# Seven-product steps in 68 of the 264 block steps of two FFN products

## The chip, the cores and the metric

The kernel runs on one core of one Trainium2 chip. The metric is the device time of one execution in microseconds. In the views of the profile PE is TensorE (matrix products), PEld its loading of the stationary operand, DVE VectorE, ACT ScalarE, POOL GpSimd, and SP the queue from which transfers are issued. PSUM is the memory in which TensorE accumulates: eight banks of 128 partitions by 512 float32.

## The reference, cut to what matters

One decoder layer on 256 tokens of 2048 features, all in float32: a feed-forward part (FFN), a token mixer, a second FFN, and a last normalization.

```python
def swiglu(h, w_in, w_out):
    gu = h @ w_in                                   # 2048 -> 2 * 5632
    gate, up = gu[..., :D_FF], gu[..., D_FF:]
    return (jax.nn.silu(gate) * up) @ w_out         # 5632 -> 2048
...
    h = h + 0.5 * swiglu(rmsnorm(h, ffn1_norm[l]), ffn1_w_in[l], ffn1_w_out[l])
    u = rmsnorm(h, mix_norm[l]) @ w_in_mix[l]
    ...                                             # pooling and gated linear attention
    h = h + jnp.concatenate([y_pool, y_gla], axis=-1) @ w_out_mix[l]
    h = h + 0.5 * swiglu(rmsnorm(h, ffn2_norm[l]), ffn2_w_in[l], ffn2_w_out[l])
return rmsnorm(h, final_norm)
```

The weights are 334 MB read once, and nearly all of the arithmetic is in the FFNs' products.

## The kernel before, in words

**A product in three matmuls.** A float32 operand is written as hi + lo, two values of a reduced float32 type (fp32r in the profile), and a product of two blocks is hi·hi + hi·lo + lo·hi, three matmuls that add up in PSUM. The activations are stationary (128 features by 128 tokens), the weights stream past them 512 columns at a time. So each pair of a 128-row tile of weights and a tile of 128 tokens costs three matmuls per 512 columns. There are two token tiles (t = 0, 1).

**Weights.** `weights` (L69) loads two row tiles (K tiles) by 512 columns, 512 KB, on SP's queue (L73); ScalarE rounds them to hi (L86, the tile `wh_...`), VectorE subtracts for lo (L87, `wl_...`); raw, hi and lo have four buffers each. `project` (L98) runs over the eight such groups of a 2048-row product, and for each group does the first token tile's six matmuls and then the second's six (L110), into one PSUM bank per token tile (`ps_acc`, four banks, so two products alternate).

**FFN in.** `ffn_in` (L210) runs over 11 chunks of 512 hidden columns: the gate product (names f1g, f2g), ScalarE's SiLU of it (L226), the up product (f1u, f2u), VectorE's gating (L234, tile `f1a`), eight TensorE transposes into the PSUM tile `f1tp` (L240, one of four banks of `ps_t`), and the split into hi (L242) and lo (L243). All 11 chunks' results are kept in SBUF.

**FFN out.** `residual` (L250) then runs, for each of four blocks of 512 output columns, over all 44 row tiles of w_out, adds half the result to the residual stream h (L262), and transposes h for the next stage; the tiles are called `wh_h`, `ps_h` here for the FFNs as for the mixer's output product. In the last block of the second FFN the last six groups are done for the first token tile first, and then for the second in halves of 256 columns, so that the final normalization of the first overlaps (`finish`, L588 to L632).

**The mixer** between the FFNs has products of the same kind (mgr, mk, mq, mv, mg, mp) with small matrix work between. It starts with the gate product mgr of 336 columns, whose result is needed for a chain of small steps before the key product mk ends.

**Order.** Each engine runs its instructions in a fixed order of its own and waits for semaphores. That order is set when the kernel is built, by a scheduler that simulates the engines' timeline and lets each engine take an instruction that is ready; the program's order is its guide. So the order in the code and the order on an engine can differ.

At the start, x comes transposed, row tile by row tile with the first weights.

## Time and profile before

| | |
|---|---|
| time, median of 3 runs | 1782.69 us (1782.53 to 1784.28) |
| profiled execution: first to last instruction (span) | 1780.9 us, 20687 instructions |
| the profiled execution's own time beside the median | its span is 1.8 us under the median |
| mean granted TensorE clock | 0.999 |
| TensorE busy | 1768.4 us, 99% |
| TensorE weight load | 1467.1 us, 82% |
| VectorE busy | 894.8 us, 50% |
| ScalarE busy | 791.2 us, 44% |
| GpSimd busy | 35.1 us, 2% |
| DMA | 338.01 MB, mean 190 GB/s; the main queue's packets took 59.5% of the engines' span |

By the chain of waits the stages are: first FFN in 4.8 to 502 us, out to 739.5; mixer to 1003.5, its output product to about 1048.6; second FFN in to 1537, out to 1772; the end to 1780.9.

A row of a group reads: source line, engine, operation, output <- inputs, partitions x elements, type, xcount | busy us, mean ns of one | idle us of the engine just before them, and what ended it. A row of the timeline or of the chain starts with the start and the length in us. Loading a weight overlaps the matmul before it, so TensorE's busy time is not the number of matmuls times the time of one alone.

### The profile page before, as it was taken

What the parts mean: (1) busy time and instruction counts of PE and PEld (TensorE: products, weight loads), DVE (VectorE), ACT (ScalarE), POOL (GpSimd) and SP (SyncE); (2) the same over time, 40 slices, a digit from 0 to 9 for tenths busy, and PEclk for the clock granted to TensorE, in tenths of its full rate; (3) what the DMA queues carried; (4) which work ended last, traced back from release to release, by engine and by line L of the source; (5) the groups of instructions that cost most, each with busy time, mean ns of one, the idle gap of its engine ahead of it and who ended that gap; (6) DMA issues with size and microseconds to landing.
All of it is one profiled execution on the core that took longest, in us unless ns stands there. A gap on an engine that the chain in (4) does not pass through costs nothing.

```text
span 1780.9 us, 20687 instructions
## 1 busy us (share of the span) xinstructions
PE 1768.4 (99%) x8086; PEld 1467.1 (82%) x8086; DVE 894.8 (50%) x902; ACT 791.2 (44%) x911; POOL 35.1 (2%) x40
## 2 busy tenths in 40 slices
PE   9999999999999999999999999999999999999998
PEld 6888888888888888878978888888888888888886
DVE  5544444444555445544455554444444555554454
ACT  6444444444444444454445544444444444443443
POOL 0000000000000000000010000000000000200000
PEclk9999999999999999999999999999999999999999
DMA  9666666666565655555554566666666666766653
GB/s 310 202 189 189 189 190 189 189 189 189 190 190 190 197 190 189 175 171 171 173 193 145 188 188 189 189 190 189 189 189 189 189 189 190 215 194 193 192 196 133
DMA packets 176449, 338.01 MB, mean 190 GB/s; under 512 B 10807, under 2 KB 19255, under 8 KB 176096
## 3 DMA queue, kind: packets, MB, share of 16 engines
q1 hardware_dynamic: 174976, 333.10, 59.5%
q0 software_dynamic: 944, 3.06, 0.6%
q8 instruction: 63, 1.03, 0.2%
q10 hardware_dynamic: 432, 0.55, 0.1%
q14 instruction: 34, 0.28, 0.0%
HBM read 334.56 MB, written 2.10 MB: 189 GB/s over the span
## 4 chain that ended last, share of the span: by engine, by line
PE 98%; issue 0%; DMA 0%; DVE 0%; ACT 0%; SPq 0%; POOLq 0%; POOL 0%; DVEq 0%
PE ps_h L110 31%; PE ps_f2g L110 13%; PE ps_f2u L110 13%; PE ps_f1u L110 13%; PE ps_f1g L110 13%; PE ps_mp L110 3%; PE ps_mv L110 2%; PE ps_mg L110 2%; PE ps_mk L110 1%; PE ps_mq L110 1%; PE ps_mgr L110 1%; PE f2tp L240 1%; PE f1tp L240 1%; PE tp_h L203 0%; DMA wr_f1g<-in_ffn_w_in 0%
## 5 line engine op out<-in xcount | busy, mean ns | idle before, releaser
L87 DVE TENSOR_TENSOR wl_h<-wr_h,wh_h 128x1024 fp32r<-128x1024 f32 x208 | 256.8, 1236 | 269.9 <-ACT wh_h L86 269.7
L86 ACT CAST wh_h<-wr_h 128x1024 fp32r<-128x1024 f32 x208 | 218.9, 1054 | 301.4 <-PE ps_h L110 274.5
L87 DVE TENSOR_TENSOR wl_f2u<-wr_f2u,wh_f2u 128x1024 fp32r<-128x1024 f32 x88 | 107.8, 1225 | 131.5 <-ACT wh_f2u L86 131.5
L87 DVE TENSOR_TENSOR wl_f1u<-wr_f1u,wh_f1u 128x1024 fp32r<-128x1024 f32 x88 | 107.8, 1225 | 129.2 <-ACT wh_f1u L86 129.1
L87 DVE TENSOR_TENSOR wl_f2g<-wr_f2g,wh_f2g 128x1024 fp32r<-128x1024 f32 x88 | 107.8, 1225 | 102.1 <-ACT wh_f2g L86 102.1
L87 DVE TENSOR_TENSOR wl_f1g<-wr_f1g,wh_f1g 128x1024 fp32r<-128x1024 f32 (+1 forms) x89 | 108.0, 1213 | 98.9 <-ACT wh_f1g L86 98.5
L86 ACT CAST wh_f2g<-wr_f2g 128x1024 fp32r<-128x1024 f32 x88 | 92.8, 1055 | 126.8 <-PE ps_f2u L110 66.6
L86 ACT CAST wh_f2u<-wr_f2u 128x1024 fp32r<-128x1024 f32 x88 | 92.7, 1053 | 122.6 <-PE ps_f2u L110 66.9
L86 ACT CAST wh_f1g<-wr_f1g 128x1024 fp32r<-128x1024 f32 (+1 forms) x89 | 93.0, 1045 | 119.1 <-PE ps_f1u L110 63.2
L86 ACT CAST wh_f1u<-wr_f1u 128x1024 fp32r<-128x1024 f32 x88 | 92.6, 1052 | 116.1 <-PE ps_f1u L110 61.9
L110 PE MATMUL ps_f1g<-wh_f1g,xT_hi 128*128 128x512 f32 x352 | 137.1, 394 | 2.5 <-ACT xT_hi L142 2.4
L110 PE MATMUL ps_h<-wh_h,f2hi 128*128 128x512 f32 (+1 forms) x364 | 139.2, 382 | 0.0
L110 PE MATMUL ps_h<-wh_h,f2lo 128*128 128x512 f32 (+1 forms) x364 | 139.1, 382 | 0.0
L110 PE MATMUL ps_h<-wl_h,f2hi 128*128 128x512 f32 (+1 forms) x364 | 139.1, 382 | 0.0
L110 PE MATMUL ps_f2g<-wh_f2g,h_hi 128*128 128x512 f32 x352 | 138.0, 392 | 0.0
L110 PE MATMUL ps_h<-wh_h,f1hi 128*128 128x512 f32 x352 | 137.3, 390 | 0.0
L110 PE MATMUL ps_h<-wl_h,f1hi 128*128 128x512 f32 x352 | 137.2, 390 | 0.0
L110 PE MATMUL ps_f2g<-wh_f2g,h_lo 128*128 128x512 f32 x352 | 137.1, 389 | 0.0
L110 PE MATMUL ps_f2g<-wl_f2g,h_hi 128*128 128x512 f32 x352 | 137.1, 389 | 0.0
L110 PE MATMUL ps_h<-wh_h,f1lo 128*128 128x512 f32 x352 | 137.0, 389 | 0.0
L110 PE MATMUL ps_f1u<-wl_f1u,xT_hi 128*128 128x512 f32 x352 | 136.9, 389 | 0.0
L110 PE MATMUL ps_f1u<-wh_f1u,xT_lo 128*128 128x512 f32 x352 | 136.9, 389 | 0.0
(225 smaller groups left out, 3323.8 us busy)
## 6 DMA issues: line engine op xcount, KB each, us to landing
wr_h<-in_ffn_w_out SPq DMA_DIRECT2D x176, 512.0 KB, 3.9
wr_f1u<-in_ffn_w_in SPq DMA_DIRECT2D x88, 512.0 KB, 3.5
wr_f2g<-in_ffn_w_in SPq DMA_DIRECT2D x88, 512.0 KB, 3.4
wr_f2u<-in_ffn_w_in SPq DMA_DIRECT2D x88, 512.0 KB, 3.4
wr_f1g<-in_ffn_w_in SPq DMA_DIRECT2D x87, 512.0 KB, 3.5
wr_h<-in_w_out_mix SPq DMA_DIRECT2D x32, 512.0 KB, 4.0
wr_mv<-in_w_in_mix SPq DMA_DIRECT2D x16, 512.0 KB, 3.6
wr_mp<-in_w_in_mix SPq DMA_DIRECT2D x16, 512.0 KB, 4.5
```

Source lines behind the costliest of these rows:

```text
L86: nc.scalar.copy(out=hi[:, :n, :cw], in_=raw[:, :n, :cw])
L87: nc.vector.tensor_tensor(out=lo[:, :n, :cw], in0=raw[:, :n, :cw], in1=hi[:, :n, :cw].bitcast(F32), op=ALU.subtract,)
L110: nc.tensor.matmul(ps[t][:, c], a[:, s], b[:, j, c], start=kt == first and i == 0, stop=kt == last and i == 2, skip_group_check=c.start > 0,)
L240: nc.tensor.transpose(tp[:, k, :], a[:, k * P : (k + 1) * P], ident)
```

## The change

**What a step is.** The FFN products are cut into steps of two token tiles (A's rows) by two K tiles by two column blocks of 512. In FFN-in the two column blocks are the gate's and the up's block of the same chunk; in FFN-out they are two neighbouring blocks of output columns. A has four blocks a(t, k), B four blocks B11, B12, B21, B22 (K tile, column block). The host lays the weights out by steps, each 1 MB in one piece, in the order B11, B12, B22, B21; `load` fetches one step, with three buffers for the raw data. Everything split out of it lies in one pool of 14 pair tiles (two blocks of 512, hi or lo).

**S and W.** An S step is the eight block products as before, 24 matmuls. A W step (the Strassen form with seven products, in Winograd's arrangement) makes sums of the blocks ahead: S1 = A21 + A22, S2 = S1 - A11, S3 = A21 - A11, S4 = A12 - S2; T1 = B12 - B11, T3 = B12 - B22, T2 = B22 - T1, T4 = B21 - T2. Its seven products, 21 matmuls, go to different places. A12·B21, S4·B22 and A22·T4 are added to the group's ordinary sums. A11·B11, S2·T2, S3·T3 and S1·T1 collect in four PSUM banks of their own over all W steps of a group; at the end of the W steps `combine` adds them up in SBUF (one ScalarE copy, four VectorE sums over 512).

The T blocks are made by VectorE in the raw tile itself, in three instructions, and all but one of the seven blocks of weights are split in pairs. The S blocks of x and of the mixer's result are made once per FFN (four K pairs); those of the hidden activations from the transposes in PSUM.

**Where.** Each FFN runs in three slabs of 4, 4 and 3 chunks: first the in-products of the slab's chunks, then the slab's part of the out-product, in two halves of 1024 columns that are added into h. In chunks 1, 3, 5, 7 and 9 the eight steps are S W S W S W W S; the out halves have 3 and 2, 3 and 2, 2 and 2 W. That makes 34 W per FFN, 68 of 264 steps.

**PSUM.** A group (one chunk's in-product, or one half of a slab's out-product) takes four banks for its sums and, if it has W, the other four for its partials; groups change sides. The transposes of a chunk go to the side of its own sums.

**The rest.** The mixer's weights come in pieces of four K tiles; mgr and mk are both done to their half first, then mgr ends, the small steps start, and mk ends. The transfers of pscale, gnorm, tri, walpha, band, w_pool and the final gains are issued on SP's queue instead of GpSimd's. In the last group of the second FFN the last two steps (four K tiles, twice as many columns) are done for one token tile first instead of the last six groups of two K tiles. At the start x comes in pairs of row tiles (256 KB) and the first step's weights in four pieces.

Names: f is the first FFN, z the second; i the in-product, o the out-product. `ps_fi3` holds the sums of chunk 3, `wr_fi3_4`, `wh_fi3_4_1`, `wl_fi3_4_1` are the raw, hi and lo data of K pair 4 (piece 1), `pw_` the partials, `add_` the combined ones. `ps_fo0_0` is the out group of the slab that starts with chunk 0, left half; `wh_fo0_2` its row pair 2. The lines below are those of the changed kernel.

```diff
+SLABS = ((0, 1, 2, 3), (4, 5, 6, 7), (8, 9, 10))
+W_PAIRS = (1, 3, 4, 6)
+PLAIN = "SSSSSSSS"
+MIXED = "SWSWSWWS"
+MIXED_CHUNKS = (1, 3, 5, 7, 9)
+OUT = {                                    # (chunk of the slab, K pair, kind), left and right half
+    4: (
+        ((0, 0, "S"), (0, 1, "S"), (1, 0, "W"), (2, 0, "S"), (1, 1, "W"), (3, 0, "S"), (2, 1, "W"), (3, 1, "S")),
+        ((0, 0, "S"), (0, 1, "S"), (2, 0, "S"), (1, 0, "W"), (3, 0, "S"), (1, 1, "W"), (2, 1, "S"), (3, 1, "S")),
+    ),
...
+}
+RAW_BUFS = 3
+UNIT_BUFS = 14
...
+    def split_to(hi, lo, src):
+        nc.scalar.copy(out=hi, in_=src)
+        nc.vector.tensor_tensor(out=lo, in0=src, in1=hi.bitcast(F32), op=ALU.subtract)
...
+    def w_step(src, name):
+        raw = load(src, name=name)
+        w = raw.rearrange("p (b c) -> p b c", c=CW)
...
+        split_to(h_hi, h_lo, w[:, 0, :])
+        b_hi, b_lo = split_pair(w[:, 2:4, :], f"{name}_1")
         nc.vector.tensor_tensor(
-            out=lo[:, :n, :cw],
-            in0=raw[:, :n, :cw],
-            in1=hi[:, :n, :cw].bitcast(F32),
+            out=w[:, 0:2, :], in0=w[:, 1:2, :].broadcast_to([P, 2, CW]), in1=w[:, 0:4:2, :],
             op=ALU.subtract,
         )
+        nc.vector.tensor_tensor(out=w[:, 2, :], in0=w[:, 2, :], in1=w[:, 0, :], op=ALU.subtract)
+        t_hi, t_lo = split_pair(w[:, 0:2, :], f"{name}_2")
+        nc.vector.tensor_tensor(out=w[:, 3, :], in0=w[:, 3, :], in1=w[:, 2, :], op=ALU.subtract)
+        u_hi, u_lo = split_pair(w[:, 2:4, :], f"{name}_3")
...
+        def w(self, a, s, b):
...
+            for (t, n), x, y in (((0, 0), a(0, 1), b["B21"]), ((0, 1), s["S4"], b["B22"])):
+                ps, start, stop = self.target(t, n)
+                three(ps, x, y, start, stop)
+            three(p16[:, 0, :], a(0, 0), b["B11"], first, last)
+            three(p75[:, 1, :], s["S1"], b["T1"], first, last)
+            three(p75[:, 0, :], s["S3"], b["T3"], first, last)
+            three(p16[:, 1, :], s["S2"], b["T2"], first, last)
+            ps, start, stop = self.target(1, 0)
+            three(ps, a(1, 1), b["T4"], start, stop)
...
+        def combine(self):
...
+            nc.scalar.copy(out=c[:, 0, :], in_=p16[:, 0, :])
+            nc.vector.tensor_tensor(out=u2, in0=p16[:, 1, :], in1=c[:, 0, :], op=ALU.add)
+            nc.vector.tensor_tensor(out=c[:, 1, :], in0=p75[:, 1, :], in1=u2, op=ALU.add)
+            nc.vector.tensor_tensor(out=d[:, 0, :], in0=p75[:, 0, :], in1=u2, op=ALU.add)
+            nc.vector.tensor_tensor(out=d[:, 1, :], in0=p75[:, 1, :], in1=d[:, 0, :], op=ALU.add)
...
+                tp = psum.tile([P, NT, 4, P], F32, tag=grp.tags[0], name=f"{name}tp{c}")
...
+    ps_r = project(hact, kd, io["w_mgr"], 336, "mgr", part=slice(0, KD // 2))
+    ps_k = project(hact, kd, io["w_mk"], CW, "mk", part=slice(0, KD // 2))
```

**How the instructions stand.** On TensorE the full matmuls go from 7272 to 7092 and the half-width ones from 138 to 90 in the program's order. Three places follow.

First VectorE in a W step's conversion. Before, in the first FFN's chunk 3 (`f1g3`, its gate product), between the low parts of the weights (`wl`) stand only the two low parts of the chunk before (`f1lo2`):

```order
L87 TENSOR_TENSOR wl_f1g3_3_1205<-wr_f1g3_3_1202,wh_f1g3_3_1204 128x1024
L87 TENSOR_TENSOR wl_f1g3_4_1223<-wr_f1g3_4_1220,wh_f1g3_4_1222 128x1024
L243 TENSOR_TENSOR f1lo2_1127<-f1tp2_0_1130,f1hi2_1126 128x4x128
L243 TENSOR_TENSOR f1lo2_1127<-f1tp2_1_1139,f1hi2_1126 128x4x128
L87 TENSOR_TENSOR wl_f1g3_5_1241<-wr_f1g3_5_1238,wh_f1g3_5_1240 128x1024
```

Now, the first W step of chunk 3 (`fi3_4`, K pair 4) and the S step `fi3_5` beside it:

```order
L109 TENSOR_TENSOR wl_fi3_4_0_1406<-wr_fi3_4_1403,wh_fi3_4_0_1405 128x512
L447 TENSOR_TENSOR flo2_1197<-ftp2_1187,fhi2_1196 128x4x128
L147 TENSOR_TENSOR wr_fi3_4_1403<-wr_fi3_4_1403 128x1024
L109 TENSOR_TENSOR wl_fi3_5_0_1372<-wr_fi3_5_1369,wh_fi3_5_0_1371 128x1024
L339 TENSOR_TENSOR sf_f2_1_1202<-a21_f2_1_1203,ftp2_1187 128x128 x2
L109 TENSOR_TENSOR wl_fi3_5_1_1376<-wr_fi3_5_1369,wh_fi3_5_1_1375 128x1024
L339 TENSOR_TENSOR sf_f2_1_1202<-sf_f2_1_1202,ftp2_1187 128x128
L339 TENSOR_TENSOR sf_f2_1_1202<-ftp2_1187,sf_f2_1_1202 128x128
L109 TENSOR_TENSOR wl_fi3_4_1_1410<-wr_fi3_4_1403,wh_fi3_4_1_1409 128x1024
L109 TENSOR_TENSOR fsolo2_1_1210<-sf_f2_1_1202,fsohi2_1_1209 128x512
L151 TENSOR_TENSOR wr_fi3_4_1403<-wr_fi3_4_1403 128x512
L109 TENSOR_TENSOR wl_fi3_4_2_1416<-wr_fi3_4_1403,wh_fi3_4_2_1415 128x1024
```

Where two subtractions over 1024 serve a step of 24 matmuls, a W step has seven instructions of which most depend on one before, and the scheduler has put an S step's and the small sums of the out-product's factors (`sf_f2`, L339) between them.

Second VectorE at the end of a group with W. Before, at the end of chunk 1, two gatings (L234) and two low parts stand among the weights' subtractions:

```order
L87 TENSOR_TENSOR wl_f1g2_2_871<-wr_f1g2_2_868,wh_f1g2_2_870 128x1024
L234 SCALAR_TENSOR_TENSOR f1a1_0_812<-ps_f1u1_0_664,rx_r_422,f1s1_0_660 128x512
L234 SCALAR_TENSOR_TENSOR f1a1_1_821<-ps_f1u1_1_665,rx_r_422,f1s1_1_662 128x512
L87 TENSOR_TENSOR wl_f1g2_3_889<-wr_f1g2_3_886,wh_f1g2_3_888 128x1024
L87 TENSOR_TENSOR wl_f1g2_4_907<-wr_f1g2_4_904,wh_f1g2_4_906 128x1024
L243 TENSOR_TENSOR f1lo1_811<-f1tp1_0_814,f1hi1_810 128x4x128
L243 TENSOR_TENSOR f1lo1_811<-f1tp1_1_823,f1hi1_810 128x4x128
```

Now, at the end of chunk 1 (the first mixed one), with the next chunk's S steps `fi2_1` to `fi2_3`:

```order
L109 TENSOR_TENSOR wl_fi2_1_0_944<-wr_fi2_1_941,wh_fi2_1_0_943 128x1024
L269 TENSOR_TENSOR add_fi1_1_818<-pw_fi1_0_600,add_fi1_0_817 128x512
L109 TENSOR_TENSOR wl_fi2_1_1_948<-wr_fi2_1_941,wh_fi2_1_1_947 128x1024
L270 TENSOR_TENSOR add_fi1_0_817<-pw_fi1_1_601,add_fi1_1_818 128x512
L271 TENSOR_TENSOR add_fi1_1_818<-pw_fi1_1_601,add_fi1_1_818 128x512
L109 TENSOR_TENSOR wl_fi2_2_0_978<-wr_fi2_2_975,wh_fi2_2_0_977 128x1024
L425 TENSOR_TENSOR ps_fi1_0_543<-ps_fi1_0_543,add_fi1_0_817 128x1024
L272 TENSOR_TENSOR add_fi1_1_818<-pw_fi1_1_601,add_fi1_1_818 128x512
L109 TENSOR_TENSOR wl_fi2_2_1_982<-wr_fi2_2_975,wh_fi2_2_1_981 128x1024
L109 TENSOR_TENSOR wl_fi2_3_0_1012<-wr_fi2_3_1009,wh_fi2_3_0_1011 128x1024
L425 TENSOR_TENSOR ps_fi1_1_544<-ps_fi1_1_544,add_fi1_1_818 128x1024
L434 SCALAR_TENSOR_TENSOR fa1_0_862<-ps_fi1_0_543,rx_r_389,fs1_0_860 128x512
```

Four sums of the partials (L269 to L272) and two additions into the sums (L425) have come in ahead of the gating (L434). TensorE, in the meantime, does 26 matmuls for the first token tile of chunk 2 (`ps_fi2_0`) before the first for the second (`ps_fi2_1`).

Third TensorE at the first out group of a slab, the left half of slab 0. Before, where one product ends and the next begins (the up product of chunk 1, the gate product of chunk 2), the three matmuls of a block product stood together and blocks in the program's order:

```order
L110 MATMUL ps_f1u1_1_665<-wh_f1u1_7_794,xT_hi3_106 128x512
L110 MATMUL ps_f1u1_1_665<-wl_f1u1_7_795,xT_hi3_106 128x512
L110 MATMUL ps_f1u1_1_665<-wh_f1u1_7_794,xT_lo3_110 128x512
L110 MATMUL ps_f1g2_0_830<-wh_f1g2_0_834,xT_hi0_103 128x512
L110 MATMUL ps_f1g2_0_830<-wl_f1g2_0_835,xT_hi0_103 128x512
L110 MATMUL ps_f1g2_0_830<-wh_f1g2_0_834,xT_lo0_107 128x512
L110 MATMUL ps_f1g2_0_830<-wh_f1g2_0_834,xT_hi0_103 128x512
L110 MATMUL ps_f1g2_0_830<-wl_f1g2_0_835,xT_hi0_103 128x512
L110 MATMUL ps_f1g2_0_830<-wh_f1g2_0_834,xT_lo0_107 128x512
```

Now, with the transposes of chunk 3 (`ftp3`) and the first W step of the group (`fo0_2`) among them:

```order
L165 MATMUL ps_fo0_0_1_1554<-wh_fo0_1_1_1595,fhi0_537 128x512
L441 MATMUL ftp3_1538<-ident_80,fa3_0_1532 128x128 x4
L165 MATMUL ps_fo0_0_1_1554<-wl_fo0_1_1_1596,fhi0_537 128x512
L165 MATMUL ps_fo0_0_1_1554<-wh_fo0_1_1_1595,flo0_538 128x512
L165 MATMUL ps_fo0_0_1_1554<-wh_fo0_2_3_1640,fhi1_877 128x512
L441 MATMUL ftp3_1538<-ident_80,fa3_1_1536 128x128 x4
L165 MATMUL pw_fo0_0_0_1644<-wh_fo0_2_0_1625,fhi1_877 128x512
L165 MATMUL pw_fo0_0_0_1644<-wl_fo0_2_0_1626,fhi1_877 128x512
L165 MATMUL pw_fo0_0_0_1644<-wh_fo0_2_0_1625,flo1_878 128x512
L165 MATMUL pw_fo0_0_0_1644<-wh_fo0_2_3_1640,fsohi1_0_890 128x512
L165 MATMUL ps_fo0_0_0_1553<-wh_fo0_4_0_1669,fhi2_1196 128x512
L165 MATMUL pw_fo0_0_0_1644<-wl_fo0_2_3_1641,fsohi1_0_890 128x512
```

Matmuls of one product no longer stand together: between those of `fo0_2` the transposes have come, and single ones of `fo0_1` and of the later step `fo0_4`, as the operands become ready by the scheduler's reckoning.

More of the change, by code (lines that the diff above doesn't have):

```diff
@@ new lines, in s_step, with block @@
+    def s_step(src, name, parts=1):
+        raw = load(src, name=name, parts=parts)
+        w = raw.rearrange("p (b c) -> p b c", c=CW)
+        pairs = [split_pair(w[:, 2 * k : 2 * k + 2, :], f"{name}_{k}", each=parts == 4) for k in range(2)]
+        def block(k, n):
+            hi, lo = pairs[k]
+            j = n if k == 0 else 1 - n
+            return hi[:, j, :], lo[:, j, :]
+        return block
+    def w_step(src, name):
+        raw = load(src, name=name)
+        w = raw.rearrange("p (b c) -> p b c", c=CW)
+        h_hi = ftmp[0].tile([P, CW], F32R, tag="half", name=f"wh_{name}_0", bufs=4)
+        h_lo = ftmp[0].tile([P, CW], F32R, tag="half", name=f"wl_{name}_0", bufs=4)
+        split_to(h_hi, h_lo, w[:, 0, :])
+        b_hi, b_lo = split_pair(w[:, 2:4, :], f"{name}_1")
@@ L173, in row_factor @@
         return rms_factor(tot, D, NT, name)
-    zeros = tmp.tile([P, CW], BF16, tag="sil", name="zeros")
-    nc.vector.memset(zeros, 0.0)
-    idle = ps_t.tile([P, CW], F32, tag="tp", name="idle")
-    for _ in range(8):
-        nc.tensor.matmul(idle, zeros[:, :P], zeros, start=True, stop=True)
     neg_half = const.tile([P, 8], F32, name="neg_half")
@@ L205, in transposed_rows @@
                     )
+            if pair is not None and pair[0](k2):
+                f = tmp.tile([P, 2, T], F32, tag="act", name=f"af_{name}_{k2}")
+                for k in range(2):
+                    nc.scalar.activation(
+                        out=f[:, k, :], in_=tp[:, k, :], func=AF.Copy, scale=cols[k2 * 2 + k]
+                    )
+                split_to(hi[:, 2 * k2 : 2 * k2 + 2, :], lo[:, 2 * k2 : 2 * k2 + 2, :], f)
+                pair[1](k2, f)
+                continue
             for k in range(2):
@@ new lines, in layer @@
+    ffn1 = ExitStack()
+    psum1 = ffn1.enter_context(tc.tile_pool(name="psum1", bufs=2, space=PSUM, reuse_waits="tile"))
+    spool1 = ffn1.enter_context(tc.tile_pool(name="spool1", bufs=1, reuse_waits="tile"))
+    ftmp[0] = spool1
+    zeros = tmp.tile([P, CW], BF16, tag="sil", name="zeros")
+    nc.vector.memset(zeros, 0.0)
+    idle = psum1.tile([P, CW], F32, tag="y", name="idle")
+    for _ in range(8):
+        nc.tensor.matmul(idle, zeros[:, :P], zeros, start=True, stop=True)
+    xT, x_s = {}, {}
```

602 lines of the change are left out of this document (417 added, 185 removed).

## Prediction

> **What bounds the kernel now.** I read the page's first part, its fourth part (the chain of waits), then the engine's own waits and the busy time by stretch.
>
> ```profile
> span 1780.9 us, 20687 instructions
> PE 1768.4 (99%) x8086; PEld 1467.1 (82%) x8086; DVE 894.8 (50%) x902; ACT 791.2 (44%) x911; POOL 35.1 (2%) x40
> ...
> PE 98%; issue 0%; DMA 0%; DVE 0%; ACT 0%; SPq 0%; POOLq 0%; POOL 0%; DVEq 0%
> ```
>
> TensorE is busy for 99% and makes up 98% of the chain that ends last. Busy alone could hide slack, since matmuls overlap, so I look at what TensorE waited for (us in total, times, longest):
>
> ```profile
> PE ps_f1g L110 <- ACT xT_hi L142: 2.4, 2, 1.4
> PE idle L180 <- DVE zeros L177: 1.2, 1, 1.2
> ```
>
> These two, both in the first 11 us, are all. Nothing else ever starved it. The chain in order of time (start, length, what) gives the pace:
>
> ```profile
> 11.73 18.90 PE ps_f1g L110 x82
> ...
> 52.40 4.76 PE ps_f1g L110 x21
> 57.16 0.87 PE f1tp L240 x8
> 58.03 17.02 PE ps_f1g L110 x75
> 75.05 21.76 PE ps_f1u L110 x96
> 96.81 4.77 PE ps_f1g L110 x21
> ```
>
> 96 matmuls in 21.76 us are 0.2267 us each, and one hidden chunk takes 96.81 - 52.40 = 44.41 us: 192 matmuls (43.52) and eight transposes (0.9). So the kernel is a count of matmuls times 0.2267 us, as long as their operands are ready. What prepares the operands has room (stretches: length, PE, PEld, DVE, ACT, POOL busy, clock, DMA share, GB/s):
>
> ```profile
> 12.00:58.03 46.03, 46.03 (x208) 38.17 (x208) 30.60 (x41) 32.45 (x51) 1.79 (x1) 1.00 0.88 301
> 58.03:102.45 44.42, 44.42 (x202) 36.88 (x201) 22.21 (x20) 19.22 (x21) 0.00 (x0) 1.00 0.61 189
> 739.54:1003.45 263.91, 263.91 (x1323) 220.94 (x1322) 136.87 (x177) 131.41 (x181) 10.22 (x12) 1.00 0.58 175
> ```
>
> In a chunk of 44.42 us VectorE works 22.21, ScalarE 19.22, and the DMA moves 189 GB/s where it reached 301 near the start.
>
> **What is removed.** An ordinary step (S) of two token tiles, two row tiles and two column blocks is 8 products of three matmuls: 24. A seven-product step (W) is 21. Each FFN has five mixed chunks with four W (20) and output groups with 3+2, 3+2 and 2+2 W (14); twice 34 is 68. 68 x 3 = 204 matmuls x 0.2267 = **-46.2 us**. The order of TensorE agrees (7272 to 7092 of the 512-column ones, 138 to 90 of the half ones), so a change that does not do what it says is excluded. At the very end 72 half-width matmuls become 24:
>
> ```profile
> 1763.38 0.28 PE L110 MATMUL ps_h<-wh_h,f2hi 128*128 128x256 f32 x1
> ...
> 1771.89 0.28 PE L110 MATMUL ps_h<-wh_h,f2lo 128*128 128x256 f32 x1
> ```
>
> 72 of them stand (1771.89 - 1763.38)/71 = 0.12 us apart; 48 fewer against 24 full ones is 24 x 0.2267 - 48 x 0.12 = **-0.3**.
>
> **What is added** stands on VectorE and ScalarE. The rows by form (busy, mean ns, then idle before):
>
> ```profile
> L87 DVE TENSOR_TENSOR wl_f2u<-wr_f2u,wh_f2u 128x1024 fp32r<-128x1024 f32 x88 | 107.8, 1225 | 131.5 <-ACT wh_f2u L86 131.5
> L87 DVE TENSOR_TENSOR wl_f1g<-wr_f1g,wh_f1g 128x512 fp32r<-128x512 f32 x2 | 1.4, 693 | 4.1 <-ACT wh_f1g L86 4.1
> L234 DVE SCALAR_TENSOR_TENSOR f1a<-ps_f1u,rx_r,f1s 128x512 f32<-128x512 f32 x22 | 15.4, 743 | 0.0
> L243 DVE TENSOR_TENSOR f1lo<-f1tp,f1hi 128x512 fp32r<-128x512 f32 x22 | 14.2, 686 | 8.7 <-ACT f1hi L242 8.7
> L425 DVE COPY_PREDICATED sT<-tri,sp 128x128 f32<-128x128 int32 x8 | 1.7, 297 | 0.0
> L86 ACT CAST wh_f2u<-wr_f2u 128x1024 fp32r<-128x1024 f32 x88 | 92.7, 1053 | 122.6 <-PE ps_f2u L110 66.9 <-PE ps_f2g L110 55.6
> L242 ACT CAST f1hi<-f1tp 128x512 fp32r<-128x512 f32 x22 | 11.8, 589 | 15.7 <-PE f1tp L240 15.7
> ```
>
> S on VectorE: two pair subtractions, 2 x 1.225 = 2.45 us against 24 x 0.2267 = 5.44 of TensorE. W: three pairs (3.68), the lone block (0.69), the broadcast subtraction over 1024 (bounded by the same 1.225) and two over 512 (2 x 0.69): 6.97 us against 21 x 0.2267 = 4.76. So during a W TensorE eats faster than VectorE cooks. A mixed chunk (4 S, 4 W) needs 9.8 + 27.9 = 37.7; its end adds four sums over 512 (2.75), two accumulator additions over 1024 (2.45; not shown before, nearest the 1225 row and twice the 686 one), two gatings (1.49) and two low parts (1.37): 45.8 us for 41.7 of TensorE (44.4 less 12 matmuls). A plain chunk needs 22.5 for 44.4. The two output groups of a slab (5 S and 3 W; 6 S and 2 W) need 40.8 and 36.3, four sums and four additions into h over 1024 (4 x 1.22) included, for 41.5 and 42.2: over a slab's last mixed chunk and these two it is 122.9 for 125.4. VectorE in all goes from 895 to about 1390 us (155 more rows over 1024, 334 over 512, 94 over 128, 40 additions into h), ScalarE from 791 to about 945 (67 more casts over 1024, 102 over 512, 38 copies): neither is the bound on average. The cover is the lead: 14 pair buffers hold the step in work, a W and part of the next. If that cover is gone, each us by which VectorE is late is a us of TensorE.
>
> I follow the worst place, the last mixed chunk of a slab and the output group behind it (S W S W S W W S, then S S W S W S W S), from the start of the chunk with the first W ready, every VectorE instruction at its full duration and the plain chunk's end ahead of it (two gatings, two low parts, one set of sums over 128: 1.49 + 1.37 + 1.9). TensorE wants the second W at 15.6, has it at 14.2; the third at 25.8, has it at 23.6; the fourth at 30.6, has it at 30.6; the output group's first W at 52.6, has it at 53.1; its later ones at 63.3 and 73.5, has them at 62.5 and 71.9. Loss: 0.5 us. The same at other prices of W: 6.4 gives 0, 7.4 gives 2.2, 8.0 gives 5.1, 8.4 gives 7.5.
>
> Which price? Downward speaks that neighbours overlap:
>
> ```profile
> 16.91 1.23 DVE L87 TENSOR_TENSOR wl_f1g<-wr_f1g,wh_f1g 128x1024 fp32r<-128x1024 f32 x1
> 18.05 0.48 DVE L143 SCALAR_TENSOR_TENSOR xT_lo<-xr,gains,xT_hi 128x256 fp32r<-128x256 f32 x1
> ```
>
> The second began 1.14 us after the first, which is listed with 1.23: 0.09 less for each of seven instructions is 6.4. Upward speaks that inside a W each of them waits for ScalarE or for the one before:
>
> ```profile
> 1774.58 0.22 DVE L612 SCALAR_TENSOR_TENSOR fin_v<-fin_v,fin_r 128x1 f32<-128x1 f32 x1 [0.68 <-POOL fin_r L611]
> 1774.84 0.16 DVE L615 SCALAR_TENSOR_TENSOR fin_r<-fin_v,fin_r 128x1 f32<-128x1 f32 x1
> ```
>
> A dependent one starts 0.04 after the end, and the waits for ScalarE in the order can cost more: seven times 0.15 would be 8.0. I take 7.2, nearer to the durations: about 1.2 us at each of the four worst places and 0.4 at each of the eight other groups with a W behind a plain one, 4 x 1.2 + 8 x 0.4 = **+8 us** (bounds 0 at 6.4, and at 8.0 4 x 5.1 + 8 x 1.8 = 35).
>
> The Trainium skill (Perfetto Trace Analysis, Optimizing Scalar/DVE Operations) says that a profiled VectorE latency is about twice its fixed cost, since the write acknowledgement overlaps with the next instruction; by that the price would be the 6.4 and this term 0. The pair of rows at 16.91 agrees with it where nothing depends.
>
> **Other edits.** Start: the first step needs 256 KB of x instead of 128 (0.5 us later), but a step of 24 matmuls asks 1.31 MB per 5.44 us, 241 GB/s, below the 301 reached. Before, chunk 0 ran from
>
> ```profile
> 4.82 1.05 PE L110 MATMUL ps_f1g<-wh_f1g,xT_hi 128*128 128x512 f32 x2
> ```
>
> to 52.40: 47.6 us for 43.5 of work, 4 lost. Now the chunk's 8 x 1.31 MB and 2.1 of x by rows take 42 us at 301 GB/s; with the 4.8 that the first product took for issue, landing and conversion the last of eight steps starts at about 46.6 instead of 43.4 (5.3 + 7 x 5.44): 3 lost. Sum **-0.5** (-3 to +2). The weights' loads move as many bytes in pieces of 1 MB with three buffers instead of four of 512 KB: nothing, hidden by a DMA at 0.61 of its share; without that cover it would be the landing time of a step. In the mixer the matmuls are the same and the gate product is opened in two halves with the key product between, as cover for the transposes of 1024 columns that now come late together. The gate product's matmuls stand at these times:
>
> ```profile
> 739.54 0.31 PE L110 MATMUL ps_mgr<-wh_mgr,h_hi 128*128 128x336 f32 x1
> ...
> 742.15 0.32 PE L110 MATMUL ps_mgr<-wh_mgr,h_lo 128*128 128x336 f32 x1
> ```
>
> (742.15 - 739.54)/17 = 0.153 us, so the cover is 48 x 0.153 + 48 x 0.2267 = 18 us, against some 10 of evacuation (four additions at 0.69, sixteen scaled halves near 0.48). The first FFN's last output group keeps its W partials waiting for PSUM banks of the transposes, with the weight buffers held: **+2.5** for both ends of the mixer (0 if the lead of the plain chunk ahead covers it, 8 if each of the four W's late partials costs its own landing of two pair subtractions, 2 us). The tail: the second token tile now follows 5.6 us behind the first (12 matmuls and 24 halves) instead of 8.6, so their chains meet, **+0.5** (0 to 2).
>
> Sum against the profiled execution: 1780.9 - 46.2 - 0.3 - 0.5 + 8 + 2.5 + 0.5 = 1744.9; the median is 1.8 above that execution (1782.69): **1747 us**.
>
> **Rivals.** (1) Everything is hidden: W at 6.4, terms 8 and 2.5 vanish: 1736. For it speaks the overlap at 16.91, against it that TensorE's order in the output groups already picks single matmuls out of five blocks, which a scheduler does when whole blocks aren't ready. (2) VectorE becomes the bound in the mixed stretches: W at 8.0, +35 instead of 8: 1774. For: seven linked instructions on two engines; against: the average of 122.9 to 125.4. (3) Slower: a group with W takes four banks for its sums and four for its partials, so the next group's first products wait until ScalarE's copy and VectorE's four sums have read the partials: 0.59 + 4 x 0.69 = 3.35 us, and behind what VectorE does first (three pair subtractions, 3.7, and two accumulator additions, 2.45): 9.5, of which the group's last S covers 5.44. Uncovered 4.1 us at 22 groups is 90; at 3 us each, 66: 1805. It decides from 1.6 us per group (1.6 x 22 = 35, all that is left of the gain). For: before, four accumulator and four transpose banks rotated; against: the new order lets TensorE do 26 matmuls for the first token tile before it needs the second partial's banks, another 5.9 us of cover.
>
> The Trainium skill (Perfetto Trace Analysis, Optimizing Tensor Performance, Matmuls) asks that independent groups rotate through different PSUM banks so that the evacuation of one overlaps the next; it speaks against this change and gives the result of the third rival. The trace of before shows no such wait, with its rotating banks, so it can't price it.
>
> **How the numbers follow.** Forecast 0.60 (1738 to 1758), rival 1 0.13, rival 2 0.15, rival 3 0.12. Below 0.2%, 3.6 us, a measurement can't tell a difference (the three runs lie within 0.1%). Faster: 0.60 + 0.13 + 0.12 of rival 2 = 0.85; same 0.03 (rest of rival 2); slower 0.12. The range reaches from rival 1 to rival 2: 1735 to 1776; what lies beyond is rival 3 and the ends of the two others, some 0.2.
>
> **What would show it.** 0.2267 us between matmuls still; TensorE busy about 1722 us and its waits, in the list, on VectorE's low parts at the fourth W of a mixed chunk and the first W of an output group, some 10 us in all; the broadcast subtraction near 1.2 us; VectorE near 1390 us. Wrong would be: waits at the first product of the second token tile in a group (rival 3), waits of the same size in every W step (rival 2), or waits for loads.

## The result

The changed kernel takes 1751.99 us (median of 4 runs, 1751.42 to 1752.49), the kernel before 1782.61 (4 runs beside it): a ratio of 0.9827, 95% interval 0.9813 to 0.984, 30.6 us less. The forecast was 1747 with a range of 1735 to 1776. The total hides that three of its terms were wrong, in opposite directions.

The page's first and fourth part of the changed kernel:

```profile
span 1749.6 us, 20543 instructions
PE 1726.8 (99%) x7858; PEld 1428.2 (82%) x7858; DVE 1324.7 (76%) x1503; ACT 912.3 (52%) x1118; POOL 24.7 (1%) x26
...
PE 97%; DVE 1%; ACT 0%; DMA 0%; issue 0%; SPq 0%; POOL 0%; POOLq 0%; DVEq 0%; ACTq 0%
```

TensorE is still the bound. VectorE went from 50 to 76% of the span. The whole list of what TensorE waited for (us in total, times, longest):

```profile
PE tp_h L367 <- DVE h_lo L287: 4.5, 1, 4.5
PE pw_fo L165 <- DVE h_lo L287: 1.8, 1, 1.8
PE ps_fi L165 <- ACT wh_fi L108: 1.7, 1, 1.7
PE idle L514 <- DVE zeros L511: 1.2, 1, 1.2
PE tp_h L367 <- DVE h L561: 1.0, 1, 1.0
PE tp_h L367 <- DVE h L878: 0.3, 1, 0.3
PE ps_fi L165 <- DVE xT_lo L287: 0.3, 1, 0.3
PE ps_fo L165 <- DVE wl_fo L109: 0.2, 1, 0.2
```

No W step waits, and no group waits for the partials' banks of the one before. What is there stands at the start and at the boundary to the mixer (`tp_h` L367 are the transposes of h there, `h_lo` L287 its low parts, `pw_fo` the partials of the last output group). A full slab, from the first product of chunk 4 to that of chunk 8, in the view by stretch (length, PE, PEld, DVE, ACT, POOL busy, clock, DMA share, GB/s), and the 25 us in which VectorE is busiest, across the two output groups of the second FFN's first slab:

```profile
1240.74:1265.74 25.00, 25.00 (x112) 20.67 (x112) 24.93 (x26) 11.57 (x13) 0.00 (x0) 1.00 0.55 196
264.53:520.60 256.07, 256.07 (x1146) 212.03 (x1146) 207.25 (x220) 132.27 (x149) 0.00 (x0) 1.00 0.57 197
```

The slab has 1113 matmuls (4 x 192 + 2 x 192 less 39 for its 13 W): 252.3 us at 0.2267, and 32 transposes of 0.11, 3.5: 255.8 of 256.07. VectorE is busy for 24.93 of the worst 25 us, and TensorE does not notice.

Where the 31.3 us of span between the two profiled executions (1780.9 and 1749.6) come from, taken from the first and last matmuls of the stages: the matmuls -46.5; the start +0.5; the boundary from the first FFN to the mixer +9.5; from the gate product to the last matmul, beyond its own matmuls, +2.0; the tail from the start of the last matmul +2.9 (from 9.0 to 11.9). These sum to -31.6, 0.3 beyond the spans, which the borders of the stages leave open.

**The boundary to the mixer.** Timeline of the changed kernel (start, length, engine, line):

```profile
718.74 1.28 DVE L561 SCALAR_TENSOR_TENSOR h<-ps_fo,h 128x512 f32<-128x512 f32 x2
719.48 1.25 PE L367 MATMUL tp_h<-ident,h 128*128 128x128 f32 x7 [1.04 <-DVE h L561]
...
720.21 3.41 DVE L109 TENSOR_TENSOR wl_mk<-wr_mk,wh_mk 128x1024 fp32r<-128x1024 f32 x3
723.55 0.86 DVE L287 SCALAR_TENSOR_TENSOR h_lo<-tp_h,gains,h_hi 128x256 fp32r<-128x256 f32 x2
725.21 1.94 PE L367 MATMUL tp_h<-ident,h 128*128 128x128 f32 x8 [4.48 <-DVE h_lo L287]
...
727.23 0.48 PE L165 MATMUL ps_mgr<-wl_mgr,h_hi 128*128 128x336 f32 x1
727.51 0.48 PE L165 MATMUL ps_mgr<-wh_mgr,h_lo 128*128 128x336 f32 x1
...
728.63 0.33 PE L165 MATMUL ps_mgr<-wh_mgr,h_hi 128*128 128x336 f32 x1
728.79 0.31 PE L165 MATMUL ps_mgr<-wl_mgr,h_hi 128*128 128x336 f32 x1
```

The last group's two column blocks end together. The first eight transposes fill both places that this side of PSUM has for them; the other eight wait until VectorE has read them, and VectorE does three subtractions of the key product's weights first. The gate product, whose operands are ready, stands behind all sixteen transposes in TensorE's order. And behind the wait its first matmuls are 0.28 us apart, from 728.63 on 0.155.

### The profile page after: what moved, and what is told of

It reads as the page before. It is cut to its first block, busy times and chain, and to the rows that moved or that the text cites. A ratio compares the mean times of both kernels' runs of the same rounds, so it can differ in the third digit from the quotient of the medians.

```text
span 1749.6 us, 20543 instructions
## 1 busy us (share of the span) xinstructions
PE 1726.8 (99%) x7858; PEld 1428.2 (82%) x7858; DVE 1324.7 (76%) x1503; ACT 912.3 (52%) x1118; POOL 24.7 (1%) x26
## 4 chain that ended last, share of the span: by engine, by line
PE 97%; DVE 1%; ACT 0%; DMA 0%; issue 0%; SPq 0%; POOL 0%; POOLq 0%; DVEq 0%; ACTq 0%
PE ps_zi L165 24%; PE ps_fi L165 23%; PE ps_zo L165 11%; PE ps_fo L165 11%; PE ps_h L165 5%; PE pw_fi L165 3%; PE pw_zi L165 3%; PE ps_mp L165 3%; PE ps_mv L165 2%; PE pw_fo L165 2%; PE pw_zo L165 2%; PE ps_mg L165 2%; PE ps_mk L165 1%; PE ps_mq L165 1%; PE ps_mgr L165 1%; PE ztp L441 1%
## 5 line engine op out<-in xcount | busy, mean ns | idle before, releaser
L109 DVE TENSOR_TENSOR wl_zi<-wr_zi,wh_zi 128x1024 fp32r<-128x1024 f32 (+1 forms) x216 | 250.6, 1173 | 106.7 <-ACT wh_zi L108 102.4
L108 ACT CAST wh_zi<-wr_zi 128x1024 fp32r<-128x1024 f32 (+1 forms) x216 | 215.7, 1012 | 217.9 <-PE ps_zi L165 150.8
L109 DVE TENSOR_TENSOR wl_fi<-wr_fi,wh_fi 128x1024 fp32r<-128x1024 f32 (+1 forms) x218 | 249.9, 1164 | 85.4 <-ACT wh_fi L108 81.1
L108 ACT CAST wh_fi<-wr_fi 128x1024 fp32r<-128x1024 f32 (+1 forms) x218 | 214.6, 1004 | 188.5 <-PE ps_fi L165 117.2
L165 PE MATMUL ps_fi<-wh_fi,xT_hi 128*128 128x512 f32 x584 | 226.8, 390 | 1.7 <-ACT wh_fi L108 1.7
L165 PE MATMUL ps_fi<-wl_fi,xT_hi 128*128 128x512 f32 x584 | 228.1, 391 | 0.1
L165 PE MATMUL ps_zi<-wl_zi,h_hi 128*128 128x512 f32 x584 | 228.0, 390 | 0.0
L165 PE MATMUL ps_zi<-wh_zi,h_hi 128*128 128x512 f32 x584 | 227.9, 390 | 0.0
L165 PE MATMUL ps_zi<-wh_zi,h_lo 128*128 128x512 f32 x584 | 227.6, 390 | 0.0
L165 PE MATMUL ps_fi<-wh_fi,xT_lo 128*128 128x512 f32 x584 | 226.4, 390 | 0.3 <-DVE xT_lo L287 0.3
```

What stands on the lines that cost most here:

```text
L108: nc.scalar.copy(out=hi, in_=src)
L109: nc.vector.tensor_tensor(out=lo, in0=src, in1=hi.bitcast(F32), op=ALU.subtract)
L165: nc.tensor.matmul(ps, x, y, start=start and i == 0, stop=stop and i == 2, **kw)
```

## The experiments

All were timed against the kernel before; differences below are against the changed kernel's 1751.99. Two medians of one and the same kernel can lie 0.6 us apart (experiment 6), so less than that says nothing.

**1. What the W steps bring together.** All 68 W become S; everything else of the change stays.

```diff
-MIXED = "SWSWSWWS"
+MIXED = "SSSSSSSS"
 OUT = {
-    4: (((0, 0, "S"), (0, 1, "S"), (1, 0, "W"), ...
+    4: (((0, 0, "S"), (0, 1, "S"), (1, 0, "S"), ...
```

> All 68 W steps become S steps; slabs, step-ordered loads, groups and mixer edits stay. Theory A (every W is hidden: TensorE pays 21 matmuls for it and nothing else): 68 x 3 x 0.2267 = 46.2 us come back, 1798 us, and the other losses that I read in the changed kernel (start, mixer boundary, tail, 15 us together) stay, less 1.8 us for the one wait of partials at the mixer boundary: 1796 to 1798. Rival B (a part of those 15 us is the price of the W's work on VectorE, spread out): 46.2 less that part, 1785 to 1793.

1794.25 us (1793.46 to 1795.2): 42.3 above, and 11.6 slower than the kernel before. So the restructuring costs 11.6 us alone, and the W steps bring 42.3 of the 46.2 that their matmuls are worth. TensorE's list in this kernel:

```profile
PE tp_h L367 <- DVE r_h_v L294: 4.1, 1, 4.1
...
PE tp_h L367 <- DVE h L561: 0.7, 1, 0.7
```

The wait at the mixer boundary is there without any W; it is not their price. Missing is the 1.8 us wait of the partials, the two waits at the boundary are 0.7 us shorter together, and the tail is 1.3 us shorter (10.6: the last matmul starts at 1782.29 of 1792.9). These are 3.8 of the 3.9 us. The time lies between the two ranges, above B's 1793 and below A's 1796: a part of the losses does come with the W, as B had it, but at the end of each FFN and not in the W steps.

**2. What a W costs VectorE, and how much more it could bear.** One more, and three more, subtractions over 1024 in each W step.

```diff
         t_hi, t_lo = split_pair(w[:, 0:2, :], f"{name}_2")
+        for _ in range(1):          # 3 in the other kernel
+            nc.vector.tensor_tensor(
+                out=t_lo, in0=w[:, 0:2, :], in1=t_hi.bitcast(F32), op=ALU.subtract
+            )
```

> In each W step the low parts of T1 and T3 are subtracted twice: one more VectorE instruction over 1024 (1.13 us by the distance of neighbours) in each of 68 steps, 77 us of work in all. Theory A (a W costs VectorE 6.3 us by the distances of its instructions, and the lead of 14 pair tiles covers it with some room): 7.5 us per W, by the recursion of the prediction 2 us at each of the four worst places and less elsewhere, 1752 to 1762. Rival C (only the average load counts, 76% now and 80% then): no change, 1751 to 1753. Rival D (VectorE already sets the pace of W steps and the 15 us lost are its waits): +77 us less what plain steps give back, over 1790.

> The same subtraction four times instead of once: 3.4 us more per W, 230 us of VectorE work, 89% of the span. Theory A: a mixed chunk then needs 55 us of VectorE for 41.7 of TensorE, an output group with three W 47.7 for 41.5; the lead gives back about 5 us per stretch, so some 8 us at each of 10 chunks and 3 at each of 12 groups: 1840 to 1880. Rival C (the average counts): 1752 to 1765. Rival D: over 1950.

1754.24 (1753.99 to 1755.3), 2.25 above, and 1824.52 (1823.12 to 1825.94), 72.5 above. 77 us of added work cost 2.25; 230 cost 72.5. One more is covered but for one place: TensorE's waits on split weights in that kernel are 2.3 us, all at the last slab's output group of the first FFN. With three more, waits appear in all groups with W, the longest of these:

```profile
PE pw_zo L169 <- ACT wh_zo L108: 6.8, 8, 1.4
PE pw_fi L169 <- ACT wh_fi L108: 5.4, 4, 2.5
```

Rival C (only the average counts) falls: VectorE is busy for 84% of that span and TensorE waits nevertheless. Rival D falls with the first kernel. Theory A stands in its direction, but it overstated the second kernel: 72 us where it had at least 88.

The price itself is in the changed kernel's timeline of VectorE:

```profile
149.15 1.22 DVE L147 TENSOR_TENSOR wr_fi<-wr_fi 128x1024 f32<-128x1024 f32 x1
150.29 1.22 DVE L109 TENSOR_TENSOR wl_fi<-wr_fi,wh_fi 128x1024 fp32r<-128x1024 f32 x1
151.42 0.48 DVE L339 TENSOR_TENSOR sf_f<-a_f,ftp 128x128 f32<-128x128 f32 x2
...
156.11 0.69 DVE L151 TENSOR_TENSOR wr_fi<-wr_fi 128x512 f32<-128x512 f32 x1
156.71 1.82 DVE L109 TENSOR_TENSOR wl_fi<-wr_fi,wh_fi 128x1024 fp32r<-128x1024 f32 x2
```

Listed with 1.22 and 0.69, they start 1.13 and 0.60 apart when nothing is waited for, the broadcast subtraction (L147) too. A W is 4 x 1.13 + 3 x 0.60 = 6.3 us, and the order puts other work between its linked instructions; no W step of this kernel makes TensorE wait. A mixed chunk then needs 4 x 2.27 + 4 x 6.33 and 7.2 for its end, 41.6 us, for TensorE's 41.7.

**3. The lead.** 12 pair tiles instead of 14.

```diff
-UNIT_BUFS = 14
+UNIT_BUFS = 12
```

> 12 pair tiles for split weights instead of 14: the lead is a W and a W, or an S and a W and one pair. Theory A (the lead covers the stretches in which a W needs 6.3 us of VectorE for 4.8 of TensorE): with less lead the mixed chunks wait, 1 to 3 us at each of 10 mixed chunks and less at the 12 output groups, 1765 to 1795. Rival C (what counts is the average load of 76%): 1751 to 1754.

1752.98 (1751.87 to 1753.97): no difference that can be told, where theory A had 13 us at least. Its trace shows two changes that nearly cancel: TensorE's waits on split weights in the first FFN's last output groups grow from 0.2 to 1.8 us, and the wait at the mixer boundary shrinks from 4.5 to 3.1. So two tiles fewer cost some 1.6 us at one place, not 1 to 3 at each of ten chunks. At 6.3 us a W the stretches need little lead; the cover was the low price more than the 14 tiles. Still smaller pools were not run.

**4. The wait at the mixer boundary: other places for the transposes.**

```diff
             transposed_rows(
...
-                psum1, grp.tags[0],
+                psum1, grp.tags[1 - i] if np_ else grp.tags[0],
             )
```

> At the end of the first FFN the transposes of the last half's two column blocks go to different sides of PSUM (the first block's to the side of the partials) instead of both to the side of the sums, where the second block's eight transposes wait until VectorE has read the first's. Theory E (the 4.5 us wait at the mixer boundary is this reuse of two PSUM places, with VectorE's low parts behind three subtractions of the next weights; with other places TensorE goes on to the gate product): 4 to 4.5 us faster, 1747.5 to 1748. Rival F (the order on VectorE decides, since the gate product needs the same low parts anyway): 0 to 1 us faster, 1751 to 1752.

1752.05 (1751.71 to 1752.53): nothing, as rival F had it, though not for its reason: the gate product's first half needs only low parts that are long done. The wait moved from the transposes to the gate product, which by the code now needs the banks that they take:

```profile
PE ps_mgr L165 <- DVE r_h_v L294: 4.7, 1, 4.7
```

**5. The same wait: VectorE's order.** The key product's first subtractions are queued behind the last low part of h.

```diff
+        last_lo[0] = nc.vector.scalar_tensor_tensor(     # in scaled_split
...
-    ps_k = project(hact, kd, io["w_mk"], CW, "mk", part=slice(0, KD // 2))
+    with tc.issue_after(last_lo[0]):
+        ps_k = project(hact, kd, io["w_mk"], CW, "mk", part=slice(0, KD // 2))
```

> VectorE's subtractions for the key product's first weights are ordered behind the last low part of h at the first mixer boundary; nothing else. Theory G (TensorE's 4.5 us wait there is VectorE's order: three subtractions, 3.4 us, stand ahead of the low parts that free the transposes' places): 2.5 to 3.4 us faster, 1748.6 to 1749.5. Rival H (ScalarE's square sums and high parts, or the places themselves, end as late): 0 to 1 us faster, 1751 to 1752.

1750.17 (1749.85 to 1751.5), 1.8 less. The wait shrinks from 4.5 to 2.5 us, between the two expectations. What is left holds the evacuation itself, ScalarE's high parts and VectorE's low parts by turns, with one of ScalarE's square sums of h (721.55) between the high parts:

```profile
721.20 0.45 ACT L287 ACTIVATE h_hi<-tp_h,gains 128x256 fp32r<-128x256 f32 x1
721.55 0.62 ACT L312 ACTIVATE sq_h<-h 128x512 f32<-128x512 f32 x1
721.68 0.48 DVE L288 SCALAR_TENSOR_TENSOR h_lo<-tp_h,gains,h_hi 128x256 fp32r<-128x256 f32 x1 [0.97 <-ACT h_hi L287]
722.16 0.82 ACT L287 ACTIVATE h_hi<-tp_h,gains 128x256 fp32r<-128x256 f32 x2
```

So VectorE's order makes 2 us of the wait. How the other 2.5 divide between the square sum (0.62 us) and the evacuation was read, not measured. No run has the gate product ahead of the transposes, which might hide all of it: in this kernel the mixer's PSUM pools are opened only behind the first FFN's.

**6. The tail: three steps held back instead of two.**

```diff
-                    hold=2 if ending and np_ == 1 else 0, by="n" if first else "t",
+                    hold=3 if ending and np_ == 1 else 0, by="n" if first else "t",
```

> In the last group of the second FFN the last three steps instead of two are done for the first token tile first, so the second tile's end follows 18 matmuls and 36 half ones (8.4 us) behind instead of 12 and 24 (5.6). From the last matmul to the end it takes 11.8 us in the changed kernel and 9.0 before. Theory I (the two tiles' final chains collide on VectorE): the tail shrinks to 9 or 9.5, 2.3 to 2.8 us faster, 1749.2 to 1749.7. Rival J (the chain of one tile has itself become longer by its sums over 512 and the read of partials): no change, 1751.5 to 1752.5.

1752.63 (1752.25 to 1753.58), 0.6 more. But the edit does nothing. Only an S step can be held back for one token tile (`w` has no such branch), and the third last step of this group is a W, `(1, 1, "W")` in the right half of the slab of three. TensorE's 7858 instructions in the two traces are the same by line, names and shapes, with 24 half-width matmuls at the end and not 36, and the tail is 11.9 us in both. So theory I stands untested, the distance was not changed, and the 0.6 us are what two medians of one kernel differ by.

**7. The tail: GpSimd's product.**

```diff
-                nc.gpsimd.tensor_tensor(out=h[t][:, s], in0=h[t][:, s], in1=gf[n], op=ALU.mult)
+                if np_ == 0:
+                    nc.gpsimd.tensor_tensor(out=h[t][:, s], in0=h[t][:, s], in1=gf[n], op=ALU.mult)
...
-            c = slice(CW, 3 * CW)
+            c = slice(2 * CW, 3 * CW)
+            nc.vector.scalar_tensor_tensor(
+                out=h[t][:, c], in0=h[t][:, c], scalar=r, in1=gf[2], op0=ALU.mult, op1=ALU.mult
+            )
+            c = slice(CW, 2 * CW)
             nc.vector.tensor_scalar_mul(h[t][:, c], h[t][:, c], r)
```

> In the last group of the second FFN GpSimd no longer multiplies the third column block by the final gains (two instructions of 1.3 us each, which stand in the tail now that the third and fourth block end together); VectorE does it in the last scaling (512 of its 1024 columns then take two operands, some 0.5 us more). Theory L (VectorE's one-element instructions beside GpSimd's product take 1.02 and 1.25 us instead of 0.15, since they can't run beside it; that and not the two tiles' collision lengthened the tail): 1.0 to 2.0 us faster, 1750 to 1751. Rival M (the tail is a fixed chain of sums, power and scaling): 0 to 1 us slower, 1752 to 1753.

1752.4 (1752.04 to 1753.0): no difference that the times can tell. The traces can. In the changed kernel a sum with one element on each of 128 partitions (L935) took 1.02 us while GpSimd multiplied, and the last step of the first tile's factor (L951) 1.25 us beside GpSimd's second product:

```profile
1734.74 1.35 DVE L915 SCALAR_TENSOR_TENSOR h<-ps_zo,h 128x512 f32<-128x512 f32 x3 [1.22 <-PE ps_zo L165]
1736.39 1.30 POOL L924 TENSOR_TENSOR h<-h,gf 128x512 f32<-128x512 f32 x1 [13.57 <-ACT sq_h L311]
1736.68 1.02 DVE L935 TENSOR_TENSOR pre<-pre 128x1 f32<-128x1 f32 x1 [0.24 <-ACT sq_h L311]
1737.75 0.28 PE L165 MATMUL ps_zo<-wh_zo,zlo 128*128 128x256 f32 x1
...
1739.68 1.25 DVE L951 SCALAR_TENSOR_TENSOR fin_r<-fin_v,fin_r 128x1 f32<-128x1 f32 x1
...
1741.76 0.75 DVE L966 TENSOR_SCALAR h<-h,fin_r 128x1024 f32<-128x1024 f32 x1
1742.42 0.15 DVE L935 TENSOR_TENSOR pre<-pre 128x1 f32<-128x1 f32 x1
```

and in the experiment 0.16 and 0.15:

```profile
1738.86 0.16 DVE L936 TENSOR_TENSOR pre<-pre 128x1 f32<-128x1 f32 x1 [0.25 <-ACT sq_h L311]
...
1739.92 0.28 PE L165 MATMUL ps_zo<-wh_zo,zlo 128*128 128x256 f32 x1
...
1741.64 0.15 DVE L952 SCALAR_TENSOR_TENSOR fin_r<-fin_v,fin_r 128x1 f32<-128x1 f32 x1
...
1743.69 0.15 DVE L936 TENSOR_TENSOR pre<-pre 128x1 f32<-128x1 f32 x1
```

The blocking was on the path. The second tile's sum (the last row of each view) stands behind the first tile's last scaling. From the start of the last matmul (1737.75 and 1739.92) to it are 4.67 us in the changed kernel and 3.77 in the experiment. Of these 0.9 us the longer scaling takes some back: the tail is 11.3 us instead of 11.9, and 11.3 again in both kernels of experiment 9, which have this edit. So theory L has the mechanism, but 0.6 us instead of 1.0 to 2.0, too little for the times to show. Rival M's time was met, but the chain is not fixed.

The rows also show why the two chains meet. The first tile's last read (1734.74) starts 3.0 us ahead of the last matmul: by the releasing matmul only two full matmuls and the 24 half-width ones come behind the first tile's end, where the forecast counted twelve and 24, or 5.6 us. Before, this distance was 8.3 us; in the kernel without W (experiment 1) it is 5.3, and the tail 10.6. That the short distance makes a part of the 2.9 us is read from these traces; no edit changed it.

**8. How many W fit.** Two W in each of the plain chunks (but the first of the first FFN), then the mixed order in all of them.

```diff
-                kinds = MIXED if c in MIXED_CHUNKS else PLAIN
+                kinds = MIXED if c in MIXED_CHUNKS else PLAIN if first and c == 0 else LIGHT
+LIGHT = "SSWSSWSS"      # "SWSWSWWS" in the other kernel
```

> The six plain chunks of each FFN get two W each (S S W S S W S S), except the first chunk of the first FFN: 22 more W, 66 matmuls or 15.0 us fewer on TensorE; VectorE gets 22 x 4.06 + 11 x 5 = 144 us more, 84% of the span. Theory A (a W costs VectorE 6.3 us, a chunk with two then needs 33.5 for TensorE's 43.0, hidden): 1737 to 1739. Rival K (the end of a group with W is free only since a group without W follows it; with W in every chunk the next group waits for the partials' banks, the third rival of the prediction): 1 to 3 us at each of 11 chunks, 1748 to 1770.

> The plain chunks get the mixed order S W S W S W W S, except the first chunk of the first FFN: 44 more W, 132 matmuls or 29.9 us fewer. A mixed chunk then needs 41.6 us of VectorE by the distances of its instructions for 41.7 of TensorE, without plain chunks to catch up; the output groups need about 38 for 41.5. Theory A: nearly hidden, 2 to 15 us of waits, 1724 to 1737. Theory A with a W at the 7.0 us of listed durations: 44.5 a chunk, 2.8 late at each of 21 chunks less what the output groups give back, 1755 to 1775.

1749.33 (1747.76 to 1751.19): 2.7 less where 22 W were worth 15.0. And 1811.63 (1806.3 to 1812.76): 59.6 more where 44 W were worth 29.9. Theory A missed in both kernels. With two W each, the new waits, 9.2 us in all, stand in the output groups, 6.3 of them in the first W behind a slab's last chunk. The longest are:

```profile
PE pw_zo L166 <- ACT wh_zo L109: 2.4, 2, 1.5
PE pw_fo L166 <- ACT wh_fo L109: 1.8, 2, 0.9
...
PE ps_fo L166 <- ACT wh_fo L109: 1.5, 1, 1.5
```

None waits for partials at the head of a group, so rival K's wait is not there, though its range holds the time. It is the place that the prediction had as the worst; that the lead is spent there is the likely reason. With the mixed order everywhere, another wait comes first:

```profile
PE ztp L442 <- DVE za L435: 15.8, 9, 2.7
PE ftp L442 <- DVE fa L435: 11.9, 5, 2.6
```

The transposes of a chunk (`ztp`, L442) stand at a fixed place in TensorE's order, and the gating that they need stands behind W work on VectorE. The chain of this kernel shows what then follows:

```profile
1147.92 1.22 DVE wr_zi L148
...
1157.94 0.60 DVE zlo L448
...
1159.70 5.87 DMA wr_zi<-in_ffn_w_in
```

The late W step gives its raw buffer back late, the next load starts late, and its 5.87 us come on top. TensorE's waits are 64 us against 11 in the changed kernel, and it is busy for 1732.8 us where 29.9 less than 1726.8 were expected: 36 us more. A part of that is the clock, which is 0.93 in the mean of this stretch:

```profile
1150.00:1175.00 25.00, 20.71 (x86) 16.12 (x85) 23.30 (x31) 14.34 (x20) 0.00 (x0) 0.93 0.42 146
```

In twelve stretches of 3.4 to 6.8 us this trace grants 0.50. TensorE is busy for 42 us in them, so half speed costs it 21 us there, against 1.7 in the changed kernel's one such stretch ahead of the tail: about 19 of the 36 us, an estimate from these figures. The other 17 were not assigned. TensorE is idle for 54 us more and busy for 36 more, less the 29.9 of matmuls: the 60.2 between the two spans, but for rounding.

**9. A better version.** Edits 5 and 7, and two, then three W only in the first plain chunk behind each slab's output groups (chunks 4 and 8, and chunk 0 of the second FFN).

```diff
+LIGHT = "SSWSSWSS"      # "SSWSWSWS" in the other kernel
...
+                kinds = MIXED if c in MIXED_CHUNKS else LIGHT if (name, c) in (
+                    ("f", 4), ("f", 8), ("z", 0), ("z", 4), ("z", 8)) else PLAIN
```

> Three edits together: the key product's first subtractions behind the low parts of h (measured alone: 1.8 us faster), the third block's gains on VectorE, and two W more in the first plain chunk behind each slab's output groups (chunks 4 and 8, in the second FFN chunk 0 too): 10 W, 30 matmuls or 6.8 us fewer on TensorE. Theory A with the loss seen at the output groups when every plain chunk had two W: these chunks lie farthest ahead of the next output group, so nearly all is kept: 1752 less 1.8, 1 to 2, and 5 to 6.8: 1741.5 to 1744. Rival N (VectorE recovers its lead only in plain chunks, wherever they lie, so that the output groups wait as they did then): 1747 to 1750.

> As the three edits together, with three W instead of two in the same five chunks (S S W S W S W S): 5 W, 15 matmuls or 3.4 us fewer on TensorE. Theory A (a chunk with three W needs 37.5 us of VectorE by the distances of its instructions for 42.3 of TensorE, and the mixed chunk behind it starts with less lead): 1739 to 1741 if the lead is whole again at the slab's output groups, which lie a mixed chunk, and mostly two chunks, farther on. Rival N (the mixed chunk behind pays): 1742 to 1746.

1742.44 (1742.18 to 1743.39) and 1739.72 (1739.63 to 1740.33): as theory A had it, and rival N falls. The second is 0.9758 of the kernel before (0.9744 to 0.9771), 42.9 us less, with 83 W. Its waits are those of the changed kernel less the 2 us at the boundary:

```profile
PE tp_h L369 <- DVE r_h_q L302: 2.5, 1, 2.5
```

So 22 more W in all plain chunks brought 2.7 us; 10 in the five chosen ones, with the two small edits, 9.5, and 15, with the same two, 12.3. The 9.5 are about what the parts give: 6.8 for 30 matmuls, 1.8 for edit 5 and 0.6 of tail for edit 7. That the place decides and not the number of W is the likely reading, since 15 cost nothing here; ten W in the other plain chunks were not run.

## Why the prediction was right in its total, and where it was not

- **The matmuls (-46.2, -0.3): right.** The distance of 0.2267 us holds in a slab of 1113 matmuls to 0.3 us, and TensorE is busy for 1726.8 us, 5 above the 1722 named. The model "a count of matmuls times 0.2267 us, as long as their operands are ready" gives the whole gain; without the W (experiment 1) 42.3 us of it are gone.
- **The price of a W (+8): wrong, it is 0.** The step that failed is "I take 7.2, nearer to the durations". The rows at 16.91 and 18.05 already showed the price of neighbours, 0.09 below the listed duration, and the forecast gave them too little weight: the 0.04 us between two one-element instructions says nothing of work that the order interleaves. The prediction's own recursion gives 0 at 6.4, so also at 6.3. The rule of the Trainium skill (Perfetto Trace Analysis, Optimizing Scalar/DVE Operations), by which the term was 0, agrees with what was measured: each listed duration overlaps the next instruction by 0.09 us.
- **"The cover is the lead": wrong as put.** Two pair tiles fewer brought 1.6 us of waits at one place and no difference in time that can be told. The first rival ("all hidden") was right on the W steps; its time of 1736 was not, because of the next two points.
- **Both ends of the mixer (+2.5, bounds 0 to 8): 11.5, outside its bounds.** The step that failed is "the cover is 48 x 0.153 + 48 x 0.2267 = 18 us, against some 10 of evacuation". The 96 matmuls are there, but TensorE's order has all sixteen transposes ahead of them, so they cover nothing; experiment 1 shows the wait without any W, experiment 4 that other places only move it, experiment 5 that VectorE's order makes 2 of its 4.5 us. The partials waiting for the transposes' banks, which the step did name, cost the 1.8 us of the list. Of the 2.0 us behind the gate product's start some 0.9 are its first six matmuls, which take 1.83 us instead of 0.93 behind the wait; the rest stays open. A cover counts only if it stands ahead of the wait in the order of the waiting engine.
- **The tail (+0.5, bounds 0 to 2): 2.9, outside too.** "Their chains meet" was right, and the trace shows it. What failed is "follows 5.6 us behind the first": the distance is 3.0 us. GpSimd's products, which the step left out, lengthen the first chain: 0.6 us of tail by experiment 7. How the rest divides stays open, since experiment 6 did not change the distance.
- **The start (-0.5): +0.5**, inside its bounds. The first product starts at 6.48 us instead of 4.82.
- **Rival 2 (VectorE bound, W at 8.0):** refuted for this kernel. One more subtraction (7.5 us a W) shows that the bound is near: 2.25 us. The recursion had about 2 at each of four places there; it was pessimistic by a factor of four.
- **Rival 3 (PSUM handoff at 22 groups):** refuted; in the changed kernel no group waits at its head for the partials before it. The wait exists: it shows twice in the kernel with the mixed order everywhere (0.4 and 0.5 us) and twice with three more subtractions (0.4 each), as TensorE waiting for `add_`, the fourth sum. The rule of the Trainium skill on rotating banks (Perfetto Trace Analysis, Optimizing Tensor Performance, Matmuls) speaks of this wait; no run here shows it at more than 0.5 us. That TensorE's 26 matmuls on the first token tile are what hides it was read from the order, not tested. The 1.8 us of the partials at the mixer are a wait for banks of another kind: there the partials wait for the transposes.
- **The named signs:** VectorE was said to come to 1390 us and came to 1324.7. Its listed durations, added up, are 1395 us; the busy time counts the overlaps once, and they are the 70 us between. The waits were said to be some 10 us in all; they were 11, at other places.

So 8 us of stalls that did not come paid for most of 9 at the mixer, 2.4 in the tail and 1 at the start; the 4.4 left over are the distance from the forecast's 1747 to 1752, less rounding. That the total came so near is luck: its terms were off by more, in both directions.
